# The second product of two FFNs by seven half-size products: operand loads run two steps ahead of their splits, PSUM tiles come from eight banks, and the side split waits longer

## The chip, the cores and the metric

One core of one Trainium2 chip. A core has a matrix engine (TensorE; PE in the profile, its weight loads PEld), a vector engine (DVE), a scalar engine (ACT), a general engine (GpSimd, POOL) and SyncE (SP), which here only issues DMA transfers. Each engine takes its instructions in the order in which they stand in its own queue. The metric is the device time of one execution in microseconds (us); lower is better. The kernel before took 2927.0 us (median of 3 runs, 2920.93 to 2932.83).

## The reference, cut to what matters

One layer of a decoder trunk on 1024 prompt tokens and 64 sample tokens, all in float32: a half-step FFN, a token mixer, a second half-step FFN, a final norm. The change touches the two FFNs:

```python
def swiglu(x, w_in, w_out):
    gu = x @ w_in                       # 1024 -> 2 * 2816
    g, u = gu[..., :D_FF], gu[..., D_FF:]
    return (jax.nn.silu(g) * u) @ w_out # 2816 -> 1024

x = x + 0.5 * swiglu(rmsnorm(x, norm_ffn1[l]), ffn1_w_in[l], ffn1_w_out[l])
mix, new_pool, new_conv, new_ssm = token_mixing(rmsnorm(x, norm_mix[l]), ...)
x = x + mix
x = x + 0.5 * swiglu(rmsnorm(x, norm_ffn2[l]), ffn2_w_in[l], ffn2_w_out[l])
```

The "second product" of an FFN is `(silu(g) * u) @ w_out`.

## The kernel before, in words

Every float32 product is made of three matmuls in the fast type `float32r`: each operand is split into a high part (ACT copies it into `float32r`) and a low part (operand minus high part, on DVE or POOL), and high x high, low x high and high x low are summed in PSUM.

An FFN's second product is done by a scheme of Strassen's kind: the tokens in two halves (`side`), the inner dimension in even and odd 128-blocks, the output in two halves, and seven products of sums of blocks in place of eight. They come in the order `ORDER2 = "4251736"`. The first product of the FFN leaves the seven sums of the hidden values in DRAM (`xq[p][kk]`, 11 blocks of 128 x 544 for each product p). `second` (L764) then does, for each p, two passes (`m0` = 0 and 2, two output blocks each). A pass takes 11 blocks kk in six weight steps of two (the sixth of one). For one step `second_weights` (L743) loads one or two blocks of `w_out` (tile `wraw`, six buffers), adds or subtracts two blocks on POOL (`ws`, L756), and splits (`wh` on ACT, L760; `wl` on DVE, L761; three buffers each). Then TensorE does 24 matmuls of 272 columns for it, 12 for the first output block (j = 0, two PSUM tiles) and 12 for the second (j = 1, two more). A pass is 132 matmuls; the two FFNs have 14 passes each.

The operands of product p+1 are fetched by the generator `fetch_x` (L767) while product p runs: a DMA into `hr` or `hp` (L776), at once behind it the split on ACT (L777) and the low part (L778) on DVE, or on POOL for the products in `LO_POOL`. Generators like this one are stepped when a clock of planned matmul time has gone far enough (`X_AT` is the delay of the first step, `X_PACE` that between steps). Before a product begins, `finish(ahead)` emits all that is left of its fetch. A scheduler sets the order on each engine's queue from what is emitted, priorities and its own estimates.

PSUM has eight banks of one tile each. In an FFN stage six carry the tag `pd` and two the tag `ps`. A pass takes its four tiles from `pd`, in turn; so its first two are those that the pass before left unused, and its last two (j = 1) are the first two of the pass before. At the end of a pass DVE adds the four tiles into the outputs (`add`, L796; 4 to 12 instructions), at a raised priority. The `ps` tiles serve transposes and norms.

`part` (L317) is a side task of the first FFN: it loads 28 weight blocks that are needed later, splits them, and stores both parts to DRAM.

Of the kernel before, what the change touches and what calls it, by code (L numbers as in the profile page):

```python
# [8 lines left out]
F32 = mybir.dt.float32  # L9
F32R = mybir.dt.float32r  # L10
I32 = mybir.dt.int32
AF = mybir.ActivationFunctionType
ALU = mybir.AluOpType
# [42 lines left out]
TURN_AT, CONST_AT = 60.0, 40.0  # L56
HP, HP_ST, HP_EV, HP_SC = 40, 0, 60, 80
SETS = (((0,), (1,), (2,), (3,)), ((0, 1), (2,), (3,)))
PART_AT, PART_W, PART_PACE = 20.0, 4.0, 3.0
NKK, NQ, NA = NFF // 2, 272, 32  # L60
ORDER2 = "4251736"
BLOCKS2 = {"1": ((0, 0), (1, 1)), "2": ((0, 1), (1, 1)), "3": ((0, 0),), "4": ((1, 1),), "5": ((0, 0), (1, 0)),
# [2 lines left out]
INTO2 = {"1": ((0, 0, 1), (1, 1, 1)), "2": ((1, 0, 1), (1, 1, -1)), "3": ((0, 1, 1), (1, 1, 1)),  # L65
         "4": ((0, 0, 1), (1, 0, 1)), "5": ((0, 0, -1), (0, 1, 1)), "6": ((1, 1, 1),), "7": ((0, 0, 1),)}
IN_PAIRS = "457"
LO_POOL = "36"
X_AT, X_PACE = 5.0, 2.2
SUM_PACE = 1.5  # L70


# [1 line left out]
def tile_hybrid_pool_ssd_macaron(  # L74
# [10 lines left out]
    V, S, T, G = nc.vector, nc.scalar, nc.tensor, nc.gpsimd  # L85
# [8 lines left out]
    def nm(s):  # L94
        uid[0] += 1
        return f"{s}_{uid[0]}"

    def act(shape=(P, 576), dt=F32, name="a"):
        return sp.tile(list(shape), dt, tag="act", bufs=N_ACT, name=nm(name))

    def pair(n, name="hl"):
        t = sp.tile([P, 2, 576], F32R, tag="pair", bufs=N_PAIR, name=nm(name))
        return t[:, 0, :n], t[:, 1, :n], t
# [16 lines left out]
    def fx(dt=F32, name="x"):  # L120
        if stage["name"] == "mix":
            return act((P, 576), dt, name)
        return stage["p"].tile([P, 592], dt, tag="fx", bufs=N_FX, name=nm(name))

    def psum(tag="ps", name="ps"):
        npd = stage["npd"]
        return stage["ps"].tile([P, 512], F32, tag=tag, bufs=npd if tag == "pd" else 8 - npd, name=nm(name))
# [18 lines left out]
    def start(gen, delay=0.0):  # L146
        c = Chain(gen, delay)
        chains.append(c)
        return c
# [13 lines left out]
    def finish(c):  # L163
        while not c.done:
            c.step()
# [8 lines left out]
    def mm(out, lhsT, rhs, start=True, stop=True, free=False):  # L174
        T.matmul(out, lhsT, rhs, start=start, stop=stop, skip_group_check=free)  # L175
        pe[0] += max(out.free_size(), 64) / 2400.0 * (1 if rhs.dtype == F32R else 4)
# [100 lines left out]
    ahead = {}  # L277
# [39 lines left out]
    def part(w, chunks, wait=PART_W, pace=PART_PACE):  # L317

        for k0, nk, c0 in chunks:
            t = fx(name="pr")[:, : nk * P]  # L320
            dma(t.rearrange("p (k c) -> p k c", c=P),
                w[k0 * P : (k0 + nk) * P, c0 : c0 + P].rearrange("(k p) c -> p k c", p=P))
            yield wait
            a = fx(F32R, "ph")[:, : nk * P]
            split(t, a, t.bitcast(F32R))
            to = [dp.tile([P, nk * P], F32, tag=nm("part"), name=nm("part")) for _ in range(2)]
            dma(to[0], a.bitcast(F32))
            dma(to[1], t)
            parted[w.tensor.name, k0, c0] = to
            yield pace  # L330

    def products(out, Wh, Wl, kk, cs, xs, k, nk):
        for ps_, (W, lo_) in enumerate(((Wh, False), (Wh, True), (Wl, False))):
# [31 lines left out]
    def split(src, hi, lo, scale=1.0):  # L365

        S.activation(hi, src, AF.Identity, scale=scale)
        if isinstance(scale, float) and scale == 1.0:
            V.tensor_tensor(lo, src, hi.bitcast(F32), op=ALU.subtract)
        else:  # L370
            V.scalar_tensor_tensor(lo, src, scale, hi.bitcast(F32), op0=ALU.mult, op1=ALU.subtract)
# [372 lines left out]
    def second_weights(wo, p, kp, n2, m0):  # L744

        raws = []
        for x, y in BLOCKS2[p]:
            raw = sp.tile([P, 4 * P], F32, tag="wraw", bufs=N_RAW, name=nm("wraw"))[:, : n2 * 2 * P]
            c0 = (4 * y + m0) * P
            dma(raw.rearrange("p (k c) -> p k c", c=2 * P),  # L750
                wo.rearrange("(k t p) c -> p t k c", t=2, p=P)[:, x, kp : kp + n2, c0 : c0 + 2 * P])
            raws.append(raw)
        with tc.high_priority(hp[0]):
            if len(raws) > 1:
                s = stage["p"].tile([P, 4 * P], F32, tag="wsum", bufs=N_S, name=nm("ws"))[:, : n2 * 2 * P]
                G.tensor_tensor(s, raws[0], raws[1], op=ALU.subtract if p in MINUS2 else ALU.add)  # L756
            else:
                s = raws[0]
            wh, wl = (sp.tile([P, 4 * P], F32R, tag=t, bufs=N_W, name=nm(t))[:, : n2 * 2 * P] for t in ("wh", "wl"))
            S.activation(wh, s, AF.Copy)  # L760
            V.tensor_tensor(wl, s, wh.bitcast(F32), op=ALU.subtract)  # L761
        return [t.rearrange("p (k c) -> p k c", c=2 * P) for t in (wh, wl)]

    def second(wo, after, half):  # L764

        X, C = {p: [] for p in ORDER2}, {}
        n = 2 * NQ  # L767

        def fetch_x(p, kks, pace):
            for kk in kks:  # L770
                if p in IN_PAIRS and kk < N_PAIR:
                    a, t, _ = pair(576, "hp")
                    t = t.bitcast(F32)
                else:
                    t, a = act((P, 576), F32, "hr"), act((P, 576), F32R, "hh")
                dma(t[:, :n], xq[p][kk])  # L776
                S.activation(a[:, :n], t[:, :n], AF.Identity)  # L777
                (G if p in LO_POOL else V).tensor_tensor(t[:, :n].bitcast(F32R), t[:, :n], a[:, :n].bitcast(F32), op=ALU.subtract)  # L778
                X[p].append((a, t.bitcast(F32R)))
                yield pace  # L780

        def residual(ms):
            for m in ms:
                for h in HALVES:
                    C[m, h] = fx(name="x")
                    dma(C[m, h][:, : NTOK[h]], xspill[h][m])
                yield 1.0

        def add(pt, m, side, c, sign):
            if side:  # L790
                to = [(1, NA + NQ * c, 0, NQ)]
            else:
                to = [(0, 0, 0, NQ)] if c == 0 else [(0, NQ, 0, NQ - NA), (1, 0, NQ - NA, NA)]
            for h, at, of, w in to:
                o = C[m, h][:, at : at + w]
                V.scalar_tensor_tensor(o, pt[:, of : of + w], 0.5 * sign, o, op0=ALU.mult, op1=ALU.add)  # L796

        finish(start(fetch_x(ORDER2[0], range(NKK - 1), 0.0)))
        ahead = None
        for at, p in enumerate(ORDER2):  # L800
            if ahead:
                finish(ahead)
            if at + 1 < len(ORDER2):
                last = at + 2 == len(ORDER2)
                ahead = start(fetch_x(ORDER2[at + 1], range(NKK), 1.6 if last else X_PACE), 14.0 if last else X_AT if at else 8.0)
            for m0 in (0, 2):
                pts = [[psum("pd", "po") for _ in range(2)] for _ in range(2)]
                for kp in range(0, NKK, 2):
                    n2 = min(2, NKK - kp)
                    W2 = second_weights(wo, p, kp, n2, m0)  # L810
                    for j in range(2):
                        for k in range(n2):
                            xh, xl = X[p][kp + k]
                            for i, (w, x) in enumerate(((0, xh), (0, xl), (1, xh))):
                                for c in range(2):
                                    mm(pts[j][c][:, :NQ], W2[w][:, k, j * P : (j + 1) * P], x[:, c * NQ : (c + 1) * NQ],
                                       start=kp + k == 0 and i == 0, stop=kp + k == NKK - 1 and i == 2)
                            tick()
                    if at == 0 and kp == 2:
                        while summing:  # L820
                            finish(summing.pop())
                        if m0 == 0:
                            finish(start(fetch_x(p, range(NKK - 1, NKK), 0.0)))
                        res = start(residual((0, 4, 1, 5) if m0 == 0 else (2, 6, 3, 7)))
                if at == 0:
                    finish(res)
                with tc.high_priority(HP_EV):
                    for j in range(2):
                        for c in range(2):
                            for y, side, sign in INTO2[p]:  # L830
                                add(pts[j][c], 4 * y + m0 + j, side, c, sign)
            if p == "7":
                after(0, [C[m, 0] for m in range(KD)])
            if p == "3" and half:
                half(1, [C[m, 1] for m in range(KD)])
        after(1, [C[m, 1] for m in range(KD)])
# [1089 lines left out]
```

## Time and profile before

| | |
|---|---|
| runs | 2927.0 us median, 2920.93 to 2932.83 |
| profiled execution | 2928.26 us, span 2925.9 us |
| TensorE busy | 2797.0 us, 96% of the span |
| second product of the first FFN | 534.4 to 801.1 us of the span |
| second product of the last FFN | 2639.9 to 2910.3 us of the span |

Of a row of waits ("PE po <- DVE x L796: 12.2, 9, 4.6") the first name is what waited, the second what ended the wait, then come the total in us, how often, and the longest. Of a row of windows the columns are: stretch and length, busy time and count on PE, PEld, DVE, ACT and POOL, the mean clock granted to TensorE (1.00 is full), the mean busy share of the DMA engines, and GB/s moved. `po` is the PSUM tile of a second product, `x<-po,x` the addition of it into an output, `hr`, `hh` and `hp` are operand tiles. A busy PE is a modelled quantity; matmuls of a full stream start about every 0.125 us.

### The profile page before, as it was taken

To read this page: it belongs to the slowest core of one execution; us is meant where nothing else is said; L and a number is where in the kernel's file an instruction comes from. 1 tells how busy PE (TensorE), PEld (TensorE's weight loads), DVE (VectorE), ACT (ScalarE), POOL (GpSimd) and SP (SyncE) were. 2 spreads that over 40 slices of the span, in tenths; PEclk is the share of its full clock that TensorE was granted. 3 is DMA by queue.
4 is the path that set the end of the run, shared out by engine and by line. 5 is a ranking of instruction groups with operands and counts; after the bars stand their busy time and mean duration, and the time that the engine had idled before them with its cause. 6 is when DMAs were issued, how large, how long until landed. Compare 5 with 4: busy or idle time off the path is not lost. (4 is left out here: it accounts for less than half of the span.)

```text
span 2925.9 us, 54651 instructions
## 1 busy us (share of the span) xinstructions
PE 2797.0 (96%) x19834; PEld 2614.9 (89%) x19834; DVE 1855.2 (63%) x2916; ACT 1395.2 (48%) x3070; POOL 1418.2 (48%) x1450
## 2 busy tenths in 40 slices
PE   7999999998999999999999999899999999999987
PEld 6999999898889999999998887678999999999987
DVE  6665555685684486866766777875665454466744
ACT  5444444443354555554556566566233434344433
POOL 6566566354542364554622333332235666663534
PEclk9999999999999999999999999999999999999999
DMA  4566633896745555543366677785775332348845
GB/s 138 187 218 208 205 119 106 272 293 191 232 126 162 162 166 181 179 146 125 101 235 220 196 233 231 252 258 178 248 236 166 101 105 94 97 134 292 279 138 166
DMA packets 515790, 539.48 MB, mean 184 GB/s; under 512 B 41780, under 2 KB 356008, under 8 KB 515512
## 3 DMA queue, kind: packets, MB, share of 16 engines
q1 hardware_dynamic: 515504, 535.99, 57.3%
q8 instruction: 156, 2.56, 0.4%
q14 instruction: 114, 0.93, 0.1%
q10 hardware_dynamic: 16, 0.00, 0.0%
HBM read 383.43 MB, written 152.65 MB: 183 GB/s over the span
## 5 line engine op out<-in xcount | busy, mean ns | idle before, releaser
L175 PE MATMUL pw<-X,wh 128*128 128x288 f32 (+2 forms) x2832 | 626.6, 310 | 3.3 <-ACT v L573 1.9
L175 PEld LDWEIGHTS pw<-X,wh 128*128 128x128 f32 x2832 | 462.2, 189 | 24.9 <-ACT v L573 2.2
L175 PE MATMUL pw<-X,wl 128*128 128x288 f32 (+1 forms) x1644 | 473.5, 288 | 0.9 <-DVE wl L456 0.9
L175 PE MATMUL pw<-hl,wh 128*128 128x256 f32 (+1 forms) x1536 | 393.2, 329 | 8.6 <-DVE t L579 5.0
L456 DVE TENSOR_TENSOR wl<-s,wh 128x512 fp32r<-128x512 f32 x288 | 240.3, 836 | 253.4 <-ACT wh L455 236.4
L449 POOL TENSOR_TENSOR s<-wraw,wraw 128x512 f32<-128x512 f32 x144 | 195.6, 1359 | 332.2 <-DVE wl L456 240.3
L175 PE MATMUL pw<-hi,wh 128*128 128x288 f32 x1120 | 332.1, 297 | 1.8 <-ACT t L611 1.7
L175 PE MATMUL pw<-hi,wl 128*128 128x288 f32 x1120 | 330.1, 295 | 0.0
L175 PE MATMUL pw<-lo,wh 128*128 128x288 f32 x1120 | 329.8, 294 | 0.0
L175 PEld LDWEIGHTS pw<-X,wl 128*128 128x128 f32 x1644 | 311.6, 190 | 1.1 <-DVE wl L456 1.1
L175 PE MATMUL pw<-hl,wl 128*128 128x256 f32 x1072 | 301.0, 281 | 0.6 <-DVE wl L456 0.6
L175 PEld LDWEIGHTS pw<-hl,wh 128*128 128x128 f32 x1536 | 259.4, 190 | 30.9 <-DVE t L579 3.5
L456 DVE TENSOR_TENSOR wl<-wraw,wh 128x512 fp32r<-128x512 f32 x216 | 179.6, 832 | 133.9 <-ACT wh L455 131.0
L455 ACT ACTIVATE wh<-s 128x512 fp32r<-128x512 f32 x288 | 181.0, 630 | 131.6 <-PE pw L175 107.5
L756 POOL TENSOR_TENSOR ws<-wraw,wraw 128x512 f32<-128x512 f32 x120 | 163.0, 1360 | 164.4 <-DMA wraw<-in_ffn_w_out_dram 93.5
L175 PEld LDWEIGHTS pw<-hi,wh 128*128 128x128 f32 x1120 | 210.8, 188 | 9.2 <-ACT t L611 3.2
L175 PEld LDWEIGHTS pw<-lo,wh 128*128 128x128 f32 x1120 | 210.8, 188 | 0.0
L175 PEld LDWEIGHTS pw<-hi,wl 128*128 128x128 f32 x1120 | 210.3, 188 | 0.3
L175 PEld LDWEIGHTS pw<-hl,wl 128*128 128x128 f32 x1072 | 203.6, 190 | 0.9 <-DVE wl L456 0.9
L455 ACT ACTIVATE wh<-wraw 128x512 fp32r<-128x512 f32 x216 | 135.3, 627 | 139.3 <-PE pw L175 123.6
L175 PE MATMUL po<-hh,wh 128*128 128x272 f32 x848 | 182.4, 293 | 11.2 <-DVE x L796 9.2
L175 PE MATMUL po<-hr,wh 128*128 128x272 f32 x848 | 178.6, 291 | 4.3 <-POOL hr L778 4.3
(401 smaller groups left out, 6870.3 us busy)
## 6 DMA issues: line engine op xcount, KB each, us to landing
wraw<-in_ffn_w_out_dram SPq DMA_DIRECT2D x240, 256.0 KB
wraw<-in_ffn_w_in_dram SPq DMA_DIRECT2D x188, 256.0 KB
wraw<-in_w_in_dram SPq DMA_DIRECT2D x144, 256.0 KB
wh<-part SPq DMA_DIRECT2D x116, 256.0 KB
wl<-part SPq DMA_DIRECT2D x116, 256.0 KB
hr<-xq SPq DMA_DIRECT2D x106, 272.0 KB
xq<-s SPq DMA_DIRECT2D x66, 272.0 KB
xq<-g SPq DMA_DIRECT2D x62, 272.0 KB
```

The source lines that it names most:

```text
L175: T.matmul(out, lhsT, rhs, start=start, stop=stop, skip_group_check=free)
L449: G.tensor_tensor(t, a, b, op=op)
L455: S.activation(wh, a, AF.Copy)
L456: V.tensor_tensor(wl, a, wh.bitcast(F32), op=ALU.subtract)
L756: G.tensor_tensor(s, raws[0], raws[1], op=ALU.subtract if p in MINUS2 else ALU.add)
```

## The change

1. `fetch_x` emits each load two steps ahead of its split (`X_LAG` = 2), and begins earlier and at a smaller pace (`X_AT` 5.0 to 4.0, `X_PACE` 2.2 to 2.0, for the first product 8.0 to 6.0; for the last 14.0 to 15.0 and 1.6 to 1.4).
2. What is left of a fetch is no longer emitted whole before its product, but step by step when the product comes to a block that is not there yet.
3. In the second pass of the first five products the tiles for j = 1 have the tag `ps` in place of `pd`.
4. The low parts of product 3 move from POOL to DVE (`LO_POOL` "36" to "6").
5. `part` waits 6.0 in place of 4.0 between load and split, and 2.0 between split and stores; a chunk then takes 9.0 of planned time in place of 7.0.

```diff
-PART_AT, PART_W, PART_PACE = 20.0, 4.0, 3.0
+PART_AT, PART_W, PART_PACE = 20.0, 6.0, 3.0
-LO_POOL = "36"
-X_AT, X_PACE = 5.0, 2.2
+LO_POOL = "6"
+X_AT, X_PACE, X_LAG = 4.0, 2.0, 2
@@ part
             split(t, a, t.bitcast(F32R))
+            yield 2.0
             to = [dp.tile([P, nk * P], F32, tag=nm("part"), name=nm("part")) for _ in range(2)]
...
-            yield pace
+            yield max(pace - 2.0, 0.5)
@@ second
-        def fetch_x(p, kks, pace):
+        def fetch_x(p, kks, pace, lag=X_LAG):
+            loaded = []
+
+            def part_x(t, a):
+                S.activation(a[:, :n], t[:, :n], AF.Identity)
+                (G if p in LO_POOL else V).tensor_tensor(t[:, :n].bitcast(F32R), t[:, :n], a[:, :n].bitcast(F32), op=ALU.subtract)
+                X[p].append((a, t.bitcast(F32R)))
+
             for kk in kks:
...
                 dma(t[:, :n], xq[p][kk])
-                S.activation(a[:, :n], t[:, :n], AF.Identity)
-                (G if p in LO_POOL else V).tensor_tensor(t[:, :n].bitcast(F32R), t[:, :n], a[:, :n].bitcast(F32), op=ALU.subtract)
-                X[p].append((a, t.bitcast(F32R)))
+                loaded.append((t, a))
+                if len(loaded) > lag:
+                    part_x(*loaded.pop(0))
+                yield pace
+            while loaded:
+                part_x(*loaded.pop(0))
                 yield pace
...
-        ahead = None
+        ahead = []
         for at, p in enumerate(ORDER2):
-            if ahead:
-                finish(ahead)
             if at + 1 < len(ORDER2):
                 last = at + 2 == len(ORDER2)
-                ahead = start(fetch_x(ORDER2[at + 1], range(NKK), 1.6 if last else X_PACE), 14.0 if last else X_AT if at else 8.0)
+                ahead.append(start(fetch_x(ORDER2[at + 1], range(NKK), 1.4 if last else X_PACE), 15.0 if last else X_AT if at else 6.0))
             for m0 in (0, 2):
-                pts = [[psum("pd", "po") for _ in range(2)] for _ in range(2)]
+                pts = [[psum("ps" if j and m0 and at < 5 else "pd", "po") for _ in range(2)] for j in range(2)]
...
                         for k in range(n2):
+                            while len(X[p]) <= kp + k:
+                                ahead[at - 1].step()
                             xh, xl = X[p][kp + k]
```

How this moves instructions stands below for two places on SP's queue, both in the first FFN. The first is the middle of product 4, the first of the seven, where the operands of product 2 are loaded. `wraw` is a weight block, `hr<-xq_0_285` to `hr<-xq_7_292` are loads of product 2's operands kk = 0 to 7, `x<-xspill` loads an output's old value. Before, from the load of product 2's third operand on:

```order
L776 DMA hr_6643<-xq_1_286 128x544
L750 DMA wraw_6787<-in_ffn_w_out_dram 128x2x256
L786 DMA x_6799<-xspill_2_85 128x512
L786 DMA x_6801<-xspill_2_93 128x576
L776 DMA hr_6678<-xq_2_287 128x544
L786 DMA x_6820<-xspill_6_89 128x512
L786 DMA x_6822<-xspill_6_97 128x576
L750 DMA wraw_6830<-in_ffn_w_out_dram 128x2x256
L776 DMA hr_6735<-xq_3_288 128x544
```

With the change, at the same two weight blocks:

```order
L784 DMA hr_6638<-xq_2_287 128x544
L784 DMA hr_6667<-xq_3_288 128x544
L784 DMA hr_6696<-xq_4_289 128x544
L751 DMA wraw_6798<-in_ffn_w_out_dram 128x2x256
L784 DMA hr_6741<-xq_5_290 128x544
L784 DMA hr_6770<-xq_6_291 128x544
L784 DMA hr_6793<-xq_7_292 128x544
L797 DMA x_6810<-xspill_2_85 128x512
L797 DMA x_6812<-xspill_2_93 128x576
L797 DMA x_6826<-xspill_6_89 128x512
L797 DMA x_6828<-xspill_6_97 128x576
L784 DMA hr_6830<-xq_8_293 128x544
```

Where kk = 1 was the last operand ahead of the first of these weight blocks, kk = 4 is now, and the second weight block, the row that follows the last one shown, comes behind kk = 8 in place of kk = 2: six more operand loads stand ahead of it.

The second place is the second pass of product 7: two `wraw` rows are one weight step (the pair of 128x256 is the pass's last), `hr<-xq_6_335` to `hr<-xq_8_337` are operands kk = 6 to 8 of product 3. Before:

```order
L750 DMA wraw_8642<-in_ffn_w_out_dram 128x2x256
L750 DMA wraw_8644<-in_ffn_w_out_dram 128x2x256
L776 DMA hr_8664<-xq_6_335 128x544
L750 DMA wraw_8681<-in_ffn_w_out_dram 128x2x256
L750 DMA wraw_8683<-in_ffn_w_out_dram 128x2x256
L776 DMA hr_8703<-xq_7_336 128x544
L750 DMA wraw_8720<-in_ffn_w_out_dram 128x2x256
L750 DMA wraw_8722<-in_ffn_w_out_dram 128x2x256
L750 DMA wraw_8759<-in_ffn_w_out_dram 128x256
L776 DMA hr_8742<-xq_8_337 128x544
L750 DMA wraw_8761<-in_ffn_w_out_dram 128x256
```

With the change, from the last operand load of product 3 (kk = 10) on; the rows wraw_8653 to wraw_8694 are the weight steps of wraw_8642 to wraw_8683 above:

```order
L784 DMA hr_8714<-xq_10_339 128x544
L967 DMA xspill_4_87<-x_6593 128x512
L967 DMA xspill_5_88<-x_6634 128x512
L751 DMA wraw_8609<-in_ffn_w_out_dram 128x2x256
L751 DMA wraw_8611<-in_ffn_w_out_dram 128x2x256
L967 DMA xspill_6_89<-x_6826 128x512
L967 DMA xspill_7_90<-x_6874 128x512
L751 DMA wraw_8653<-in_ffn_w_out_dram 128x2x256
L751 DMA wraw_8655<-in_ffn_w_out_dram 128x2x256
L751 DMA wraw_8692<-in_ffn_w_out_dram 128x2x256
L751 DMA wraw_8694<-in_ffn_w_out_dram 128x2x256
```

All of product 3's operands now stand ahead of these weight steps, and no operand load is left between them.

## Prediction

> **What bounds the kernel now.** I read the page first, then the two stages that the diff touches in windows, pass by pass, then the waits of TensorE (PE) in them, then the timeline at the longest wait.
>
> ```profile
> span 2925.9 us, 54651 instructions
> PE 2797.0 (96%) x19834; PEld 2614.9 (89%) x19834; DVE 1855.2 (63%) x2916; ACT 1395.2 (48%) x3070; POOL 1418.2 (48%) x1450
> ```
>
> PE is busy 96%, so only its idle time and its slow time can be won. The windows below are the two second products, then product 5 of the first FFN (two passes), then five single passes that are long.
>
> ```profile
> core 0: us, PE busy (x) PEld busy (x) DVE busy (x) ACT busy (x) POOL busy (x), PEclk, DMA share, GB/s
> 534.37:801.07 266.70, 245.11 (x1863) 239.94 (x1862) 170.86 (x276) 103.52 (x179) 130.10 (x101) 0.98 0.79 254
> 2639.90:2910.27 270.37, 253.74 (x1904) 247.48 (x1903) 161.36 (x268) 97.74 (x180) 121.87 (x94) 0.96 0.69 225
> 607.87:641.30 33.43, 33.43 (x267) 33.43 (x265) 24.77 (x44) 14.20 (x24) 17.33 (x13) 1.00 0.94 301
> 552.08:572.36 20.28, 17.45 (x135) 16.84 (x133) 11.00 (x25) 7.85 (x13) 1.54 (x2) 1.00 1.06 370
> 660.61:681.50 20.89, 18.55 (x134) 18.06 (x133) 10.69 (x19) 7.94 (x13) 13.49 (x11) 0.92 0.84 271
> 699.50:724.77 25.27, 19.76 (x132) 19.14 (x133) 9.73 (x16) 6.60 (x12) 5.77 (x5) 0.86 0.36 111
> 2656.84:2680.01 23.17, 20.00 (x134) 19.51 (x133) 11.61 (x26) 7.85 (x13) 2.48 (x2) 0.85 1.06 368
> 2804.36:2830.21 25.85, 20.19 (x132) 19.56 (x133) 9.70 (x15) 5.32 (x10) 6.08 (x7) 0.80 0.37 109
> ```
>
> Product 5 runs without a gap at full clock: 33.43 / 2 = 16.72 us a pass, the floor. Fourteen passes make 234.0 us; the two stages take 266.7 and 270.4, so 32.7 + 36.4 = 69.1 us are above the floor. That is all that this change can reach there. What PE waits for, in products 4, 2, 5, 1, 7 of the first FFN, the same of the last, then products 3 and 6 of the first and of the last:
>
> ```profile
> PE po L175 <- DVE x L796: 12.2, 9, 4.6
> PE po L175 <- DVE wl L761: 2.3, 2, 1.4
> PE po L175 <- ACT wh L760: 0.7, 2, 0.5
> ...
> PE po L175 <- DVE x L796: 10.1, 9, 4.5
> PE po L175 <- DVE wl L761: 2.1, 4, 1.1
> PE po L175 <- ACT wh L760: 0.7, 1, 0.7
> ...
> PE po L175 <- POOL hr L778: 1.9, 2, 1.0
> ...
> PE po L175 <- POOL hr L778: 2.4, 4, 1.1
> PE po L175 <- ACT hh L777: 0.6, 1, 0.6
> ```
>
> The largest is PE waiting for L796, the emptying of a PSUM tile: 22.3 us in the first five products. It falls at the 13th matmul of a pass, the first into the tiles for j = 1, which are the first two of the pass before. The longest, in product 7's second pass, shows why DVE is late:
>
> ```profile
> 700.33 0.41 SPq L776 DMA_DIRECT2D hr<-xq  x1
> ...
> 703.02 0.41 SPq L776 DMA_DIRECT2D hr<-xq  x1
> ...
> 704.02 0.66 ACT L777 ACTIVATE hh<-hr 128x544 fp32r<-128x544 f32 x1 [4.54 <-DMA hr<-xq]
> 704.58 1.14 ACT L760 ACTIVATE wh<-ws 128x512 fp32r<-128x512 f32 x2
> ...
> 705.23 1.41 DVE L761 TENSOR_TENSOR wl<-ws,wh 128x512 fp32r<-128x512 f32 x1 [4.07 <-ACT wh L760]
> 706.56 1.60 DVE L796 SCALAR_TENSOR_TENSOR x<-po,x 128x272 f32<-128x272 f32 x6
> ...
> 707.04 1.52 PE L175 MATMUL po<-hp,wh 128*128 128x272 f32 x4 [4.56 <-DVE x L796]
> ```
>
> ACT stands 4.54 us at a split whose load was issued 3.7 us earlier; the weight split waits behind it on ACT, DVE waits for that, and the additions wait behind DVE's weight split. So a late operand of the next product stops the present one.
>
> **The change, part by part.**
>
> *Eight banks.* With `ps` tiles for j = 1 in the second passes, a first pass takes tiles emptied a pass before, and a second pass takes two idle `pd` and two `ps`: through product 7, the additions have a whole pass (16.7 us) to finish. The 22.3 us of waits go. Not all is gain, since a PE that does not wait there may wait for the next thing. In product 4's second pass that is the weights:
>
> ```profile
> 555.92 0.39 PE L175 MATMUL po<-hp,wh 128*128 128x272 f32 x1 [2.17 <-DVE x L796]
> 556.84 0.36 PE L175 MATMUL po<-hp,wh 128*128 128x272 f32 x1 [0.53 <-DVE x L796]
> ...
> 2661.36 0.59 PE L175 MATMUL po<-hp,wh 128*128 128x272 f32 x1 [2.84 <-DVE x L796]
> 2662.28 1.02 PE L175 MATMUL po<-hp,wh 128*128 128x272 f32 x3 [0.32 <-DVE x L796]
> ...
> 556.00 0.38 SPq L750 DMA_DIRECT2D wraw<-in_ffn_w_out_dram  x1
> ...
> 561.88 0.63 ACT L760 ACTIVATE wh<-wraw 128x512 fp32r<-128x512 f32 x1 [1.62 <-DMA wraw<-in_ffn_w_out_dram]
> ...
> hr<-xq SPq DMA_DIRECT2D x106, 272.0 KB
> ```
>
> There the DMA engines are full (share 1.06, 370 GB/s), and the fourth weight step, issued at 556.00, is split at 561.88, while without waits PE would want it at 552.1 + 3 x 3.0 = 561.1. The change puts six more operand loads ahead of that block: 6 x 272 KB at 370 GB/s = 4.4 us at most. So I count this pass's waits (2.17 + 0.53 + 2.84 + 0.32 = 5.9 us) as not won. Bounds: all 5.9 won, or 4.4 - 2.7 = 1.7 and 4.4 - 3.2 = 1.2 us lost in the two calls. I take none, between them. Term: 22.3 - 5.9 = **16.4 us**.
>
> *Clock.* The passes with long waits show a granted clock of 0.92 to 0.80, those without 1.00. What a pass costs beyond the floor and its waits is the slow clock: in the first FFN product 1's second pass 20.89 - 16.72 - 2.4 = 1.8 and product 7's 25.27 - 16.72 - 5.8 = 2.8; in the last FFN product 7's 25.85 - 16.72 - 5.6 = 3.5 (waits from the timeline; each is part of the rows above). Sum **8.1 us**, gone with the waits. Product 4's in the last FFN (23.17 - 16.72 - 3.2 = 3.3) I keep, with its waits. The Trainium skill, "TensorE: Matmul & The Clock Gate", Part 1, says that the gate falls to half after an idle window of about 3.4 us; by that alone only the 4.6 and 4.5 us waits of product 7 would count and the term would be 6.3. The 0.92 of the pass with a longest wait of about 2 us speaks against it.
>
> *Loads two steps ahead.* The wait of ACT for `hr` goes where load and split are two paces (4.0 us of planned time) apart: above, 3.7 us would have done. At product 7 the loads of product 3 now stand ahead of the pass altogether. The waits for `wl` and `wh` sum to 2.3 + 0.7 + 2.1 + 0.7 = 5.8 us; product 2's 1.38 below and small ones in products 4 and 2 are not of that kind; I take **3.7 us** for product 7, bounds 0 and 5.8. Products 3 and 6: in the last FFN the waits for `hr` and `hh` are 3.0 us, and the order moves those loads up by as much as ten weight steps; I take **2.4 us** (bounds 0 and 3.0 + 1.7 of slow clock). In the first FFN (1.9 us) the last loads move by two steps at most: 0.
>
> *New waits for weights.* In the new order DVE has split one weight step in place of two ahead of the additions at the end of product 5's first pass and of product 1's and 3's second passes. Where that was so before, at the end of product 4's second pass, PE then waited 1.38 us in the first FFN:
>
> ```profile
> 578.38 0.52 PE L175 MATMUL po<-hh,wl 128*128 128x272 f32 x2 [1.38 <-DVE wl L761]
> ```
>
> and 0.2 in the last. Three places, two FFNs, bounds 0 and 6 x 1.4 = 8.3; I take **-2.0 us**, near the lower, since additions now wait for no late split.
>
> *Low parts of product 3, and `part`.*
>
> ```profile
> L778 POOL TENSOR_TENSOR hr<-hr,hh 128x544 fp32r<-128x544 f32 x22 | 30.9, 1404 | 41.3 <-ACT hh L777 40.8 <-DVE wl L761 0.5
> L778 DVE TENSOR_TENSOR hr<-hr,hh 128x544 fp32r<-128x544 f32 x29 | 23.5, 815 | 22.7 <-ACT hh L777 22.7
> ...
> PE pw L175 <- ACT wh L455: 1.1, 1, 1.1
> PE pw L175 <- DVE wl L456: 0.6, 1, 0.6
> ```
>
> Eleven low parts cost DVE 11 x 0.82 = 9.0 us in product 7, where it is busy 9.73 of 25.27 us: hidden; uncovered, it would be 9.0 us a call. POOL loses 15.4 us of work there, which helps `ws`. The side task takes 28 x 2 = 56 us longer; its last store moves from behind the 78th to behind the 97th of the 104 weight loads of that stage, so it still ends ahead of the second product. PE waits for split weights in that stage 1.7 us in all. I take 0, bounds -2 and +1.7.
>
> Sum: 16.4 + 8.1 + 3.7 + 2.4 - 2.0 = 28.6 us, against the profiled execution's own 2928.26: 2899.7. That execution lies 1.3 us above the median, well inside the spread of the runs, so I forecast **2900 us**.
>
> **The rivals.** *A: the gain is whole.* Product 4 gives its 5.9 + 3.3, product 6 the rest (2.3), no new waits (2.0): 28.6 + 13.5 = 42 us, 2886. For it: product 5 and both passes around it run at the floor at 301 GB/s. Against it: the full DMA engines in product 4.
>
> *B: the wait only changes its name.* PE next waits for weights in all passes as I assume for product 4; only the chain of product 7 (4.6 + 4.5 + 2.8 + 3.5 = 15.4 us) is cured, by the loads, and the new waits take 2 to 8 us of it: 2918. For it: the weight splits run only one or two steps ahead. Against it: in the passes without PSUM waits, the same queues keep up. The Trainium skill's same page, in the section on HAM oscillation, tells of a kernel to which PSUM double-buffering "gave no further gain"; by that, the time would be B's.
>
> *C: slower.* The operand loads now stand in bunches ahead of the weights on SP's queue. If the 4.4 us of product 4 recur at each of the six products that fetch for the next, in both FFNs, 12 x 4.4 = 53 us go against 28.6 + 5.9 = 34.5 won: 2947. It decides from eight of the twelve on. Against it: elsewhere the DMA share is 0.36 to 0.94, so a bunch finds room.
>
> **How the numbers follow.** Forecast (2892 to 2911) 0.52, A (below 2892) 0.20, B (2911 to 2926) 0.21, C 0.07. A measurement of this kernel can tell about 0.5%, 14.6 us, from no change: faster is then below 2912.4. That is the forecast, A and little of B: 0.74; same 0.19; slower 0.07. The range leaves out C, the top of B and the bottom of A, some 0.2 together: 2884 to 2921.
>
> **What would show it.** Right: the waits of `po` for L796 in products 4 to 7 fall from 22.3 us to under 2; product 7's second pass lasts under 18 us at clock 1.00 in both FFNs; ACT no longer stands 4.5 us at `hh<-hr`; the two stages last about 252 and 256 us. Product 4's second pass keeps over 2 us of waits, now for weights. Wrong: waits for `wl` or `wh` above 10 us in the two stages (B), or weight loads that land later in products 5 to 7 (C), or a first product of the first FFN that grows by over 3 us.

## The result, and the profile after

The changed kernel takes 2909.1 us (median of 6 runs, 2904.98 to 2910.03), the kernel before beside it 2925.6 us (6 runs, 2920.40 to 2932.83): a ratio of 0.994, 95% interval 0.9924 to 0.9957. 2900 was forecast: 16.5 us are won of 28.6. The page of the changed kernel begins:

```profile
span 2908.2 us, 54642 instructions
PE 2790.9 (96%) x19834; PEld 2613.8 (90%) x19834; DVE 1867.1 (64%) x2938; ACT 1396.1 (48%) x3070; POOL 1396.3 (48%) x1428
```

The span is 17.7 us shorter, but not where I had placed it. The windows of the changed kernel below are the two second products, then five stretches of them: product 4's second pass (first FFN), product 7's first and second pass (first FFN), product 4's second and product 7's first pass (last FFN).

```profile
core 0: us, PE busy (x) PEld busy (x) DVE busy (x) ACT busy (x) POOL busy (x), PEclk, DMA share, GB/s
528.20:794.49 266.29, 246.38 (x1863) 242.75 (x1862) 186.09 (x292) 102.41 (x178) 124.79 (x96) 0.96 0.79 255
2627.48:2892.64 265.16, 249.02 (x1904) 245.40 (x1903) 160.45 (x279) 97.37 (x179) 108.72 (x83) 0.97 0.70 230
544.90:569.80 24.90, 18.87 (x134) 18.02 (x132) 12.78 (x28) 9.96 (x16) 1.83 (x2) 0.93 1.05 361
673.00:699.50 26.50, 19.85 (x135) 19.31 (x134) 10.25 (x22) 5.22 (x11) 9.71 (x8) 0.81 0.63 195
699.50:716.20 16.70, 16.70 (x134) 16.70 (x133) 6.04 (x14) 4.78 (x9) 0.64 (x1) 1.00 0.31 94
2645.20:2669.80 24.60, 19.07 (x135) 18.35 (x134) 13.37 (x29) 9.79 (x16) 2.12 (x2) 0.93 1.05 365
2773.10:2798.60 25.50, 19.26 (x133) 18.83 (x133) 10.14 (x22) 5.19 (x9) 9.68 (x8) 0.87 0.57 181
```

The stages last 266.3 and 265.2 us, against 266.7 and 270.4 before: 5.6 us less, where 29 were forecast. Product 7's second pass is cured (25.3 and 25.9 us before, 16.7 now). But its first pass now lasts 26.5 and 25.5 us (18.0 and 19.9 before, by the starts of their matmuls), at a clock of 0.81 and 0.87, and product 4's second pass has grown by 4.6 and 1.4 us. What TensorE waits for in products 4, 2, 5, 1, 7 of the first and of the last FFN, now complete lists:

```profile
PE po L175 <- ACT wh L761: 10.2, 4, 4.2
PE po L175 <- DVE wl L762: 3.8, 3, 2.5
...
PE po L175 <- ACT wh L761: 9.9, 6, 3.3
PE po L175 <- DVE wl L762: 3.9, 3, 3.0
```

No wait for a PSUM tile is left there (22.3 us before). Waits for split weights have taken their place: 10.2 + 3.8 + 9.9 + 3.9 = 27.8 us, against 5.8 before. The longest stands in product 7's first pass; ACT's timeline ahead of it:

```profile
669.12 0.61 ACT L761 ACTIVATE wh<-ws 128x512 fp32r<-128x512 f32 x1
672.35 0.66 ACT L774 ACTIVATE hh<-hr 128x544 fp32r<-128x544 f32 x1 [2.62 <-DMA hr<-xq]
674.44 0.66 ACT L774 ACTIVATE hh<-hr 128x544 fp32r<-128x544 f32 x1 [1.43 <-DMA hr<-xq]
679.17 0.66 ACT L774 ACTIVATE hh<-hr 128x544 fp32r<-128x544 f32 x1 [4.08 <-DMA hr<-xq]
679.74 1.65 ACT L761 ACTIVATE wh<-ws 128x512 fp32r<-128x512 f32 x3
```

Three operand splits of product 3 stand in a row between two weight splits. Each waits for its own load; from the end of one weight split (669.73) to the next (679.74) ACT needs 10.0 us, 8.1 of them waiting. TensorE uses up a full weight step, two of a pass's eleven blocks, in 16.72 x 2 / 11 = 3.0 us. Behind it, on PE and DVE:

```profile
680.40 1.27 PE L175 MATMUL po<-hp,wh 128*128 128x272 f32 x4 [4.18 <-ACT wh L761]
684.15 0.82 PE L175 MATMUL po<-hp,wl 128*128 128x272 f32 x2 [2.48 <-DVE wl L762]
...
679.86 0.72 DVE L775 TENSOR_TENSOR hr<-hr,hh 128x544 fp32r<-128x544 f32 x1 [4.01 <-ACT hh L774]
680.50 3.00 DVE L807 SCALAR_TENSOR_TENSOR x<-po,x 128x272 f32<-128x272 f32 x10
683.42 2.42 DVE L762 TENSOR_TENSOR wl<-ws,wh 128x512 fp32r<-128x512 f32 x3
```

TensorE waits 4.18 us for ACT. Then it waits 2.48 us for DVE, which first makes up ten additions (3.0 us) that stood behind the low part of that operand. It is the chain of before with another last link, and none of the three operands was needed for 40 us. The clock followed it down:

```profile
673.00:678.60 5.60, 3.22 (x26) 3.00 (x24) 1.58 (x3) 0.67 (x2) 1.70 (x1) 1.00 0.83 231
678.60:688.80 10.20, 5.92 (x24) 5.60 (x25) 5.98 (x14) 2.33 (x5) 4.04 (x3) 0.50 0.55 193
```

The rest of the gain lies outside the second products. One piece is real and was forecast as nothing: the stretch of the first FFN in which `part` splits its first blocks. The window over the same 498 matmuls in the kernel before, then in the changed one:

```profile
151.90:229.50 77.60, 74.35 (x498) 69.08 (x497) 47.83 (x78) 34.20 (x83) 43.80 (x44) 1.00 0.67 214
```

```profile
152.20:226.30 74.10, 73.72 (x498) 69.09 (x497) 44.06 (x74) 33.41 (x78) 44.82 (x45) 1.00 0.61 196
```

TensorE's waits in it, before and after:

```profile
PE pw L175 <- DVE t L579: 1.6, 2, 0.9
PE pw L175 <- ACT wh L455: 1.1, 1, 1.1
PE pw L175 <- DVE wl L456: 0.6, 1, 0.6
```

```profile
PE pw L175 <- DVE wl L457: 0.4, 1, 0.4
```

The waits fall from 3.3 to 0.4 us, the stretch by 3.5 us. Over a longer stretch of that first product, the 2200 matmuls from about 104 us on, the gain is larger: 337.6 us before, 330.7 now. The other piece, 6.7 us between the first second product and the token mixer's end, looks like scatter of one execution: that stretch took 1362.7 us in the profile of before, 1357.2 in another execution of the same kernel, and 1352.8 to 1358.1 in all later profiles.

### The profile page after: what moved, and what is told of

Read it like the earlier page. It is cut to its first block, busy times and chain, and to the rows that moved or that the text cites. A ratio compares the mean times of both kernels' runs of the same rounds, so it can differ in the third digit from the quotient of the medians.

```text
span 2908.2 us, 54642 instructions
## 1 busy us (share of the span) xinstructions
PE 2790.9 (96%) x19834; PEld 2613.8 (90%) x19834; DVE 1867.1 (64%) x2938; ACT 1396.1 (48%) x3070; POOL 1396.3 (48%) x1428
## 5 line engine op out<-in xcount | busy, mean ns | idle before, releaser
L175 PEld LDWEIGHTS pw<-hl,wh 128*128 128x128 f32 x1536 | 259.0, 189 | 24.7 <-ACT t L578 2.9
L175 PE MATMUL pso<-yhl,wh 128*128 128x288 f32 (+1 forms) x768 | 177.8, 337 | 5.4 <-ACT acc L1727 4.5
```

## The experiments

In the table, "stages" is the sum of the two second products in the profiled execution, "first FFN" the length of the 498-matmul stretch. Ratios are to the kernel before on the same chip, with 95% intervals.

| kernel | median, us | ratio | stages, us | first FFN, us |
|---|---|---|---|---|
| before (first profile, and e8) | 2925.6; 2920.7 | | 537.1; 536.5 | 77.6; 78.1 |
| changed | 2909.1 | 0.994 (0.9924 to 0.9957) | 531.5 | 74.1 |
| e1: before + banks | 2910.4 | 0.995 (0.9934 to 0.9966) | 528.3 | 78.6 |
| e2: e1 + `part` | 2908.4 | 0.9944 (0.9926 to 0.9962) | 523.6 | 74.0 |
| e3: changed, `part` undone | 2916.4 | 0.9977 (0.9967 to 0.9988) | 531.7 | 78.5 |
| e4: changed, banks undone | 2908.6 | 0.9952 (0.9934 to 0.9969) | 528.1 | 74.2 |
| e5: changed, splits pinned | 2887.4 | 0.9879 (0.9859 to 0.9899) | 511.0 | 74.0 |
| e6: e5, loads later at product 4 | 2889.3 | 0.9882 (0.9863 to 0.9901) | 509.2 | 74.4 |
| e7: e5, banks undone | 2889.8 | 0.9887 (0.987 to 0.9904) | 511.7 | 74.0 |
| e9: e5, lag 0 | 2895.4 | 0.9905 (0.9888 to 0.9923) | 510.2 | 74.4 |
| e10: e5, lag 4 | 2886.4 | 0.9872 (0.9856 to 0.9887) | 508.4 | 73.9 |
| e11: e5, bunches of four, lag 4 | 2901.2 | 0.9927 (0.9913 to 0.9941) | 524.2 | 73.9 |
| e12: changed, lag 0 | 2893.9 | 0.991 (0.9896 to 0.9923) | 511.3 | 74.6 |

### Parts of the change alone: e1 to e4 and e8

My theory at first: ACT, standing at operand splits whose loads have not landed, is the common cause, and banks only move where it shows. The rival: the banks carry the gain.

e1 gives the kernel before the eight banks and nothing else; the order on ACT, DVE, POOL and SP stays.

```diff
-                pts = [[psum("pd", "po") for _ in range(2)] for _ in range(2)]
+                pts = [[psum("ps" if j and m0 and at < 5 else "pd", "po") for _ in range(2)] for j in range(2)]
```

> The kernel before with item 3 alone (ps tiles for j = 1 in the second passes of the first five products); every engine's order is as before, so only waits for PSUM tiles can change. Theory T1 (the eight banks are worth what I priced, and the change's new operand order gives part of it back): the 22.3 us of waits for L796 in products 4 to 7 fall under 2, product 4's second pass and product 7's second pass keep 1 to 3 us of waits for weights each, the 7.0 us stall of the first pass of product 7 that the changed kernel shows is absent, and the time is 20 to 26 us below before, that is below the changed kernel: ratio to before 0.991 to 0.993. Rival T2 (a PE that does not wait for PSUM waits for weights in any order): 5 to 10 us below before, ratio 0.9965 to 0.998.

Its waits in products 4 to 7 of the first, then of the last FFN, complete:

```profile
PE po L175 <- ACT wh L760: 5.9, 7, 1.6
PE po L175 <- DVE wl L761: 5.2, 6, 2.1
...
PE po L175 <- DVE wl L761: 6.6, 9, 1.5
PE po L175 <- ACT wh L760: 5.0, 6, 1.6
```

The 22.3 us of PSUM waits are gone, the 5.8 us of weight waits have grown to 22.7. The stages gain 8.2 us on e8, a third of the 24.5 us that I had put on the banks and the clock. The ratio, 0.995, lies between the ranges of the two theories (0.991 to 0.993 and 0.9965 to 0.998): the waits behave as T2 says, but the whole gain is larger than T2's, and larger than what the stages show.

e2 adds the longer waits of `part` to e1; e3 takes them out of the changed kernel.

```diff
-PART_AT, PART_W, PART_PACE = 20.0, 4.0, 3.0
+PART_AT, PART_W, PART_PACE = 20.0, 6.0, 3.0
...
+            yield 2.0
...
-            yield pace
+            yield max(pace - 2.0, 0.5)
```

> The kernel before with items 3 and 5 (eight banks, side task with longer waits), operand loads as before. The profiles of before and after differ by 6.2 us ahead of the first second product (534.4 against 528.2 us). If item 5 makes that (T1), this kernel is 4 to 7 us faster than eight banks alone and its first second product begins at 527 to 530 us; if it is scatter of single executions (rival), the two agree within 2 us.

> The changed kernel with item 5 undone. By T1 4 to 7 us slower than the changed kernel (about 2914, ratio to before 0.996); by the rival (scatter) no change, ratio 0.994.

In the table the 498-matmul stretch is 77.6 to 78.6 us in all four profiles with the old `part`, and 73.9 to 74.6 in the ten with the new: 4 us, with no overlap. Over the 2200 matmuls it is 335.4 to 338.4 against 330.2 to 331.4 us: about 6 us, with no overlap either. By the ratios the piece is worth 2 us (e1 to e2, intervals overlapping) to 11 us (e3 to the changed kernel). The traces show a part of that difference: in e2, which has no lag, 200 matmuls further on take 3.1 us longer than in e1, and in the changed kernel they do not (see e9). The 11 us are more than the traces locate.

e4 takes the banks out of the changed kernel.

```diff
-                pts = [[psum("ps" if j and m0 and at < 5 else "pd", "po") for _ in range(2)] for j in range(2)]
+                pts = [[psum("pd", "po") for _ in range(2)] for _ in range(2)]
```

> The changed kernel with item 3 undone: new operand order, six pd banks. By T1 the waits for L796 come back at about 15 to 22 us on top of the new order's waits for weights: 2920 to 2932, ratio to before 0.998 to 1.002. By T2 the weights are the limit either way and it stays near the changed kernel: 2909 to 2914, ratio 0.994 to 0.996.

Its waits in the same products:

```profile
PE po L175 <- ACT wh L761: 6.0, 3, 2.7
PE po L175 <- DVE x L807: 5.9, 6, 3.0
...
PE po L175 <- DVE x L807: 5.8, 7, 3.0
PE po L175 <- ACT wh L761: 4.5, 3, 2.5
PE po L175 <- DVE wl L762: 0.7, 1, 0.7
```

PSUM waits come back (11.7 us) and weight waits shrink (27.8 to 11.2); time and stages are those of the changed kernel (528.1 and 531.5 us). In this order the banks are worth nothing.

e8 is the kernel before once more, for the scatter of a single profile.

> The kernel before, unchanged, for a second profile. The four profiles of this study so far have the stretch from the end of the first second product to the last w_o matmul at 1353 to 1356 us, the profile of before 1362.7, though nothing of the change lies there but the order of a few rows. If that is scatter of one execution, this profile has 1352 to 1358 us there and a span of about 2918; the stretch ahead of the first second product is 533 to 536 us again.

Its stages (267.1 and 269.4 us) repeat those of the first profile; its stretch up to the token mixer's end does not (1357.2 us, above). Its first second product begins at 531.4 us, ahead of the 533 to 536 expected, so the start scatters by some 3 us too.

### Loads really ahead of the splits: e5, e6, e7

The lag of two loads stands in the source, but hardly in the order: from the issue of an operand load to the start of its split it is 5.4 us in the median before and about 6 us after (5.8 to 6.1, by how loads and splits are paired). Where ACT waits for a load, its split starts mostly 4 to 6 us after the issue, at most 7.6. The scheduler had moved the splits up again. e5 forbids that for the ACT split alone.

```diff
-                S.activation(a[:, :n], t[:, :n], AF.Identity)
+                cut = S.activation(a[:, :n], t[:, :n], AF.Identity)
+                if p != ORDER2[0]:
+                    tc.keep_in_program_order(cut)
```

> The changed kernel with one line more: each operand split on ACT, except those of the first product, is kept behind everything that was written ahead of it for ACT, so that the scheduler cannot move it up to its load. In the changed kernel the median time from issue of an operand load to its split is 6.1 us, before 5.4, and ACT waits 102 us for operand loads, before 138. Theory T3 (PE's waits of 3 to 4 us for wh and wl in the first pass of product 7 are ACT standing at an operand split in front of the weights): with the splits held back ACT waits under 40 us for operands, the first pass of product 7 falls from 26 us to under 19 in both FFNs, and the time is 8 to 16 us below the changed kernel, ratio to before 0.989 to 0.992. Rival T4 (it is the weights' own transfers or the ten additions on DVE that hold PE there): the pass stays over 22 us, ratio 0.993 to 0.996.

The two second products of e5, then products 2, 5, 1 and 7 of the first FFN together, and product 4's second pass:

```profile
527.00:782.60 255.60, 243.60 (x1863) 241.66 (x1862) 185.46 (x293) 101.13 (x178) 123.87 (x96) 0.97 0.82 266
2614.50:2869.90 255.40, 245.73 (x1904) 242.88 (x1903) 167.91 (x279) 97.23 (x179) 109.34 (x83) 0.99 0.73 238
569.80:703.30 133.50, 133.50 (x1056) 133.50 (x1056) 102.32 (x172) 54.05 (x95) 62.52 (x46) 1.00 0.85 274
544.00:569.80 25.80, 19.82 (x134) 19.34 (x134) 13.61 (x29) 10.28 (x17) 2.74 (x2) 0.87 1.04 358
```

1056 matmuls, eight passes, without one gap: 133.5 / 8 = 16.7 us a pass. The stages are 20.5 us shorter than in the changed kernel, and 2887.4 us beat both kernels, by more than the 8 to 16 us that T3 gave. In products 4 to 7 12.3 of the changed kernel's 27.8 us of weight waits are left, in products 4 and 2. What is left above the floor is mostly product 4's second pass (25.8 and 24.7 us, where the DMA engines are full) and product 6.

e6 starts the fetch for product 2 later and spaces the loads of the old outputs, to thin out that burst.

```diff
-                yield 1.0
+                yield 1.0 if 0 in ms else 2.4
...
-X_AT if at else 6.0))
+X_AT if at else 16.0))
```

> As the last, and the loads in product 4 are spread: product 2's fetch begins at 16.0 in place of 6.0, and the old output values for the second pass are fetched 2.4 in place of 1.0 apart. Theory T5 (product 4's second pass, 24.9 us in the changed kernel, waits for weights that stand behind a bunch of loads): it falls under 20 us in both FFNs and product 2 gains at most 2 us a call, so 5 to 12 us below e5, ratio 0.986 to 0.990. Rival (the DMA engines have the same bytes to move by the end of product 2, so the waits move into product 2, and the scheduler's order there has no weight step ahead of the additions of that pass): product 2's first pass grows by as much, within 3 us of e5.

Product 4's second pass falls to 20.9 and 21.7 us, but product 2's first grows from 16.7 and 17.8 to 20.3 and 20.2. The time is e5's: the stages gain 1.8 us, less than the scatter. The bytes only wait elsewhere.

e7 takes the banks out of e5, by the diff of e4.

> e5 with item 3 undone (six pd banks). If late operand splits were the cause of most PSUM waits too (T6, since DVE's additions stand behind weight splits that stand behind them), the waits for L796 in products 4 to 7 stay under 10 us in all and the time is 0 to 6 us above e5. If the banks are worth what I priced them at (T1), the waits are 15 to 22 us and the time 12 to 25 us above e5.

The waits for a PSUM tile come to 3.2 us in both FFNs together, the stages to 511.7 us. With ACT on time six banks are enough. In the stages of single profiles the banks were thus worth 8.2 us in the old order, -3.4 in the changed one, 0.7 here.

### Is it the distance, or the place? e9 to e12

e5 changed two things at once: a split came later behind its load, and it kept its place among the weight splits. e9 and e10 vary the lag of e5.

```diff
-        def fetch_x(p, kks, pace, lag=X_LAG):
+        def fetch_x(p, kks, pace, lag=0):
```

> e5 with the lag taken back to 0: each operand load is followed at once by its split in the written order, and ACT keeps that order. It tells whether e5 won by the distance from a load to its split, or only because the splits were nailed to fixed places among the weight splits. Landing theory: ACT stands at the splits again for most of a landing (4 to 6 us), its waits for operand loads in products 2 to 6 rise from 28 us to over 80 in the two FFNs, some of the passes of products 2, 5, 1, 7 are above 16.72 us again, and the time goes back to 2900 to 2915 (ratio 0.992 to 0.998). Place theory: the order alone does it, the two second products stay at 254 to 258 us and the time at 2886 to 2891 (ratio 0.987 to 0.989).

> e5 with a lag of 4 loads in place of 2. Landing theory: with 2 loads (two paces of 2.0 us) the splits of products 5 and 7 came 10 to 17 us behind their loads, those of the others 6 to 8 us, against landings of 4 to 6; four loads leave some 4 us more, so ACT's waits for operand loads fall from 28 us to under 10, but the passes of products 2, 5, 1, 7 already run at 16.72 us, so the time gains 0 to 3 us on e5: 2884 to 2888 (ratio 0.986 to 0.988), unless the later splits of the last operands are themselves late for TensorE (product 3's and 6's first passes grow; then 2888 to 2895). Place theory makes the same of it within what can be told apart.

e10's time is as expected (ACT's waits for operand loads fall to 13 us, not quite to the 10), and its 2886.4 us can't be told from e5. With e9 my theory fell. ACT's waits for operand loads in products 2 to 6 are 109 us, more than the changed kernel's 102; yet the stages last 252.4 and 257.8 us, as short as e5's:

```profile
531.53:783.93 252.40, 241.45 (x1863) 237.63 (x1862) 174.32 (x285) 99.82 (x175) 118.36 (x87) 0.99 0.83 270
2618.11:2875.89 257.78, 246.87 (x1904) 243.19 (x1903) 162.13 (x279) 97.60 (x180) 109.45 (x83) 0.99 0.72 236
```

In product 7's two passes ACT stands 16.2 us at such splits and TensorE does not wait at all. So it is not how long ACT stands in sum.

The time of e9, 2895.4 us, lies above the 2886 to 2891 of the place theory. e9 and e5 differ by 8 us in time, and by 6.1 us in their profiles, none of it in the stages: 4.5 us lie in the first FFN ahead of them. One operand of product 4 is loaded early there, and ACT stands at its split:

```profile
464.76 0.66 ACT L774 ACTIVATE hh<-hr 128x544 fp32r<-128x544 f32 x1 [8.42 <-DMA hr<-xq]
```

TensorE then waits 1.56 us for a weight split on ACT and 0.58 us for one on DVE, and its clock is lower (0.95 in the mean of the stretch). The 200 matmuls around it, from about 450 us on, take 33.0, 34.1 and 34.5 us in e2, e9 and e12, the three runs with the new `part` and no lag; ACT stands 8.4 to 8.9 us at that split in each. In all other profiles they take 29.9 us. Here the lag helps, by 3 to 5 us.

The new theory: a weight split is made 4.6 us or more ahead of its first matmul, when nothing disturbs. ACT's standing costs only what is above this slack *between two weight splits*. In the changed kernel the scheduler had put up to three operand splits into one such gap (4 threes, 9 twos, 25 ones from product 2 on in the first FFN), and their waits add up; in e9 (45 ones) and in the kernel before (42) it is mostly one. In the kernel before, two long waits came within 9 us of each other, ahead of product 7's second pass and in it: the 4.54 us at 704.02 that the prediction shows, and this one:

```profile
695.57 0.66 ACT L777 ACTIVATE hh<-hr 128x544 fp32r<-128x544 f32 x1 [5.09 <-DMA hr<-xq]
```

e11 makes long rows, but of landed loads; e12 undoes the lag in the changed kernel with nothing pinned, which gives rows of one again.

e11:

```diff
-        def fetch_x(p, kks, pace, lag=X_LAG):
+        def fetch_x(p, kks, pace, lag=4):
...
-                yield pace
+                yield pace * 4 if kk in (3, 7, NKK - 1) else 0.0
             while loaded:
                 part_x(*loaded.pop(0))
-                yield pace
+                yield 0.0
```

> e5 with the operands of the next product fetched in bunches of four (four loads at once, then four paces of nothing) and split four at once, a lag of 4 behind: ten or so times in a second product ACT now has four splits in a row between two weight splits, all of loads that landed long before. Slack theory (new, from e9: a pass is delayed only where ACT's standing between two weight splits is longer than the 4.6 us by which it splits a weight ahead of its use; four splits of landed loads take 4 x 0.6 = 2.4 us): products 5, 1 and 7 stay at 16.72 us a pass, the two second products at 252 to 258 us, 2884 to 2892 (ratio 0.986 to 0.989). Bunch theory (it is the bunches of the changed kernel in themselves, up to three splits in a row, with DVE's low parts bunched too): several passes of 5, 1, 7 grow to 18 to 25 us, 2896 to 2912 (ratio 0.990 to 0.996).

e12:

```diff
-X_AT, X_PACE, X_LAG = 4.0, 2.0, 2
+X_AT, X_PACE, X_LAG = 4.0, 2.0, 0
```

> The change with its lag taken back to 0 and nothing pinned: eight banks, the new paces, LO_POOL and part stay. Slack theory: with the split written right behind its load, the scheduler puts mostly one split between two weight splits (40 ones, 6 twos, 2 longer in the last twelve products' halves, against 25, 9 and 4 in the changed kernel), so ACT still stands for 90 to 110 us in all but seldom over 4.6 us in one place: product 7's first pass falls from 26 us to under 19, the two second products sum to 510 to 520 us (531.5 in the changed kernel), and the time is 2892 to 2901 (ratio 0.989 to 0.992). Rival (only the distance of a split from its load helps, so a lag of 0 is no better than the changed kernel's 2): 2905 to 2915 (ratio 0.993 to 0.997).

e11, products 5, 1 and 7 of the first and of the last FFN:

```profile
609.80:710.10 100.30, 100.30 (x794) 100.30 (x793) 74.07 (x127) 40.21 (x72) 41.49 (x32) 1.00 0.79 256
2703.40:2803.70 100.30, 100.30 (x795) 100.30 (x794) 71.53 (x126) 39.27 (x70) 42.17 (x33) 1.00 0.75 245
```

Six passes at 16.72 us in each: four splits in a row cost nothing when their loads have landed. The total missed the slack theory's range all the same: 2901.2 us against 2884 to 2892, inside the bunch theory's 2896 to 2912, though the passes that this theory named did not grow. Against e5 the stages are 13.2 us longer, and 10.3 of these lie in product 2's first pass (20.0 and 19.3 us, against 16.7 and 17.8) and product 3's second (21.6 and 19.2, against 18.0 and 17.3). With bunches the first and last operands of a fetch come later, but I did not follow it further.

e12, its two stages, then product 7's first pass, and ACT in it:

```profile
534.66:788.18 253.52, 242.25 (x1863) 237.78 (x1862) 179.30 (x286) 100.73 (x176) 116.47 (x88) 0.99 0.83 269
2622.05:2879.85 257.80, 245.81 (x1904) 241.80 (x1903) 165.53 (x279) 97.90 (x180) 108.98 (x83) 0.99 0.72 236
677.60:695.10 17.50, 17.28 (x134) 16.80 (x133) 12.30 (x22) 6.21 (x11) 8.04 (x6) 1.00 0.84 266
```

```profile
684.55 0.66 ACT L774 ACTIVATE hh<-hr 128x544 fp32r<-128x544 f32 x1 [3.52 <-DMA hr<-xq]
685.12 0.61 ACT L761 ACTIVATE wh<-ws 128x512 fp32r<-128x512 f32 x1
...
688.94 0.40 ACT L761 ACTIVATE wh<-ws 128x256 fp32r<-128x256 f32 x1
693.51 0.66 ACT L774 ACTIVATE hh<-hr 128x544 fp32r<-128x544 f32 x1 [4.16 <-DMA hr<-xq]
694.07 0.62 ACT L761 ACTIVATE wh<-ws 128x512 fp32r<-128x512 f32 x1
```

ACT stands as long at one split as in the changed kernel (4.16 against 4.08 us), 119 us in all against 102. But a weight split follows each operand split, the widest gap between two of them in this pass is 4.7 us in place of 10.0, and the pass lasts 17.5 us in place of 26.5. Without its lag the change takes 2893.9 us: 0.991 against 0.994, the stages 20.2 us shorter, 17.1 of it in product 7's two first passes. Ahead of the stages e12 pays 4.6 us for the missing lag (see e9). So the lag, the piece that I counted as a gain, is what took the rest of the gain away.

The bound of 4.6 us is not shown. In e12, a stretch without any wait of TensorE (655 to 677 us) has this:

```profile
666.62 0.66 ACT L774 ACTIVATE hh<-hr 128x544 fp32r<-128x544 f32 x1 [5.09 <-DMA hr<-xq]
```

e9 has a wait of 5.14 us that costs nothing either, and in the changed kernel a gap of 6.6 us between two weight splits (645.7 to 652.4, with 4.8 us of waiting) is not followed by a wait of TensorE; the gap of 10.0 us is. A full weight step lasts 3.0 us on TensorE, so a gap eats into the lead only with what it lasts beyond that, and the next gap finds what is left of the lead. That fits these cases; where the bound lies was not measured.

## Why the prediction was right, and where it was wrong

The forecast range holds the time, and the sign is right. That is luck in good part: of the 28.6 us forecast for the two stages, the profile shows 5.6 there; about 6 came from `part`, priced at nothing. Of the signs named for it, the waits for L796 and product 7's second pass came out as said, the two stages did not; and the sign named against it, over 10 us of waits for split weights, came with 27.8.

**The floor** of 16.72 us a pass, reached in every pass of products 5, 1 and 7 in e5 and e11, and in all but one in e10, and the 69 us above it were the right frame.

**Eight banks, 16.4 us.** The waits for L796 in products 4 to 7 went from 22.3 us to nothing, as the first test said; the gain did not follow. The step that failed is "the 22.3 us of waits go", with only product 4 left out of it: what TensorE waits for next was asked for one pass, and answered with 2.0 us for all the others. e1 shows it in an unchanged order: 22.3 us of PSUM waits less, 16.9 us of weight waits more. That is the mechanism of rival B, to which I gave 0.21, though its time of 2918 us did not come. The Trainium skill's "no further gain" from PSUM double-buffering ("TensorE: Matmul & The Clock Gate", the section on HAM oscillation), told of a kernel for few rows after its loop had been put in another order, agrees with e4 (-3.4 us in the stages) and e7 (0.7), and not with e1 (8.2).

**Clock, 8.1 us.** Product 7's second pass lost its slow clock, its first pass took it over (0.81 and 0.87).

**Loads two steps ahead, 3.7 + 2.4 us.** This is the step that was wrong in sign. I reasoned with planned times ("two paces apart, 4.0 us"), and took the order of the source for that of ACT's queue. On the queue the distance grew by about half a microsecond, the last of product 3's splits still stood 4.08 us, and the rows of three were more (4 in place of 1 in the first FFN). By e12 the piece costs 20.2 us in the stages. The places of the order that I argued from were on SP's queue, where the loads did move up, and not on ACT's, where the wait was.

**New waits for weights, -2.0 us, bounds 0 and 8.3.** I priced places by a row of DVE's order, at most 1.4 us each. Of the 27.8 us measured, 15.5 go when the splits are pinned on ACT (e5), so more than half come from ACT's order, which the bounds did not contain; product 7's first pass alone lost 8.5 and 5.7 us.

**Product 4's second pass** was counted as neither won nor lost, with up to 1.7 and 1.2 us of loss; it lost 4.6 and 1.4 (3.4 and 3.1 against e8). Its two longest waits in the first FFN have two causes. Ahead of 554.16 TensorE waits 3.02 us behind a row of five operand splits, at which ACT stands 5.9 us. Ahead of 560.80 it waits 1.91 us for a weight split on ACT that itself waits 3.82 us for its weight block, while the DMA engines are full (share 1.05). e6 thins the burst and the pass falls to 20.9 us, though the sum gains nothing.

**Low parts and `part`, 0 us, bounds -2 and +1.7.** `part` gave 4 us in the 498 matmuls and about 6 us in the 2200, above the bound: I had looked only at the waits for split weights there, and not at those for L579, an addition on DVE that stood behind `part`'s work. e12 against e2 holds the new paces, the fetch step by step and the low parts of product 3 together: 12.3 us in the stages, not separated.

By the profiles, then: banks, paces and low parts, without the lag, take the stages from 537 to 511 us (e12), the lag gives 20 of these 26 back, and `part` gives about 6 ahead of them. That is 12 of the 17.7 us between the two profiled spans; most of the rest lies in the stretch up to the token mixer's end, which only the first profile has so long (1362.7 us). By the ratios the lag costs less, about 9 us (0.991 against 0.994). With the lag held in place (e5, e10) the time is about rival A's 2886 us, and e7 shows that the banks are not what it takes.

## What to carry to other kernels

Where an engine in order splits both the operand needed now and the one needed later, ask for each gap between two of the first kind how long it can last: the sum of the waits in it, against the time by which the first kind still runs ahead after the gaps before it. A lag between a load and its use is only there if it is in the engine's queue; where a scheduler may move the use up, read the order on the engine that waits, and pin the use. More buffers behind a late engine rename its wait; once the engine is on time, try taking them out again.

## What the runs showed of the hardware that was not expected

A 272 KB operand load mostly took 4 to 6 us (2.9 to 7.6 in the changed kernel) from issue to the split that waited for it, at 255 GB/s in the mean of the stage. The Trainium skill ("DMA: Bandwidth & Descriptors", the section on the anatomy of one DMA) gives about 2.0 us and the bytes over 436 GB/s for a transfer issued on the GpSimd path; by that one alone would take 2.6 us, an estimate. These loads are issued from SP, among others of the same queue, and no run here tells apart what makes the difference, so the measured time is the one to plan a lag by. The same page's rule for kernel authors, to issue early and wait late, is what e5 and e10 do; e9, which does not, has stages as short (510.2 us).

The clock fell to 0.50 at 678.6, 2.4 us into a wait of 4.18 us, and stayed there for 10.2 us, 5.9 of them busy. A shorter wait, of 3.02 us in product 4's second pass, was followed by the same: 1.5 us after its end the clock fell to 0.50, from 555.7 to 559.1 us.
